# A mixture-of-experts layer in split fp32: one first-layer piece unsplit for light experts, another order of experts, longer rows in the second-layer loads

## The chip, the cores and the metric

One core of a Trainium2 chip runs the whole layer in one launch. The metric is the device time of one execution in microseconds (us), the median of three runs. TensorE (PE) multiplies, VectorE (DVE) and ScalarE (ACT) work on elements, GpSimd (POOL) issues indirect transfers, SyncE (SP) issues the weight loads.

## The reference, cut to what matters

The layer mixes 512 tokens of width 1024 (state-space heads and pooling heads), and then sends each token through 4 of 32 experts. Everything is fp32, and the 384 MiB of expert weights are read once.

```python
logits = xt @ router_w + router_b            # 512 tokens, 32 experts
top_val, top_idx = lax.top_k(logits, 4)
gates = softmax(top_val)
# for each expert e, on the tokens sent to it:
hb = x @ w1[e] + b1[e]                       # 1024 -> 2048
g = minimum(hb[..., ::2], 7);  u = clip(hb[..., 1::2], -7, 7)
act = g * sigmoid(1.702 * g) * (u + 1)       # 1024
y = (act @ w2[e] + b2[e]) * gate             # 1024 -> 1024, added into the token's row
x = x + g2 * sum_of_y;  out = rmsnorm(x, final_norm_w)
```

## The kernel before, in words

**Split products.** An fp32 product is made of reduced fp32 (F32R) ones. A piece of weights, a tile `raw` of 128x2048 and 1 MiB, is split by `ring_split` (L1070): ScalarE rounds it to `hi` (L1076), VectorE subtracts, `lo = raw - hi` (L1077). There are three hi/lo pairs. The tokens of an expert are split in the same way. `prod` (L1299) multiplies 128 rows of weights: hi·hi, lo·hi and hi·lo, on four PSUM halves of 512 columns in the first layer and on two in the second.

**Light and wide experts.** The kernel ranks the experts by their number of tokens at run time (`order`, L1427). Positions 0 and 1 hold experts 0 and 1 with 128 slots each; the other positions follow `RANK` (L48), and `CAPS` (L50) gives the slots of each. Ranks 15 to 29 are light, 64 slots (`LT`): their 64 hi columns and 64 lo columns stand side by side in one stationary operand of 128 columns, so `prod` needs two products where a wide expert (80 to 128 slots) needs three. Rows 64 to 127 of the result hold what the lo columns gave; `rest` (L1273) copies them to `b2h`, and a product with the strip `slt` adds them, along with the bias, to rows 0 to 63 (`bias1` L1281, `bias2` L1291). Position `MID` (16) holds the fullest expert, rank 0, with a block of 128 and one of 64 slots; it runs in a branch of its own, without overlap with its own second layer. All others alternate wide and light after the first three.

**The loop over positions** (L1523). At position p: eight pieces of the first layer, `w1_piece(e, k)`, each 128 rows of 8192 bytes. Ahead of the second piece, the second-layer bias and the scatter of position p-2 (`end`); behind the third, the gather and transposition of the next expert's rows (`next_x`). Then `selector(p)` writes the one-hot columns that pick the expert's row of the biases: for a wide expert a tile `sel` of 128x128, `SELB` (2) buffers; for a light one the strip `slt`, of which columns 0 and 2 serve the first-layer bias, column 1 the second-layer bias, column 3 the rest. Then the bias and `swiglu` (L1308: Gelu on ACT to `sg`, clamp on DVE to `su`, product to `act`), with which the four PSUM halves (two tiles A, two buffers in all) come free for the next first layer. Between them, in `C` (L1344), the second layer of position p-1 in four loads `w2_pair(e, kk)`: rows 256kk to 256kk+127 in the left half of the tile, the next 128 in the right half, so a partition gets two rows of 4096 bytes. Last, `act` is transposed by PE, eight blocks of 128 columns (L1109 light, L1119 wide), for the second layer one position later.

**Buffers and queues.** The loads go through a ring of 11 `raw` buffers, in order, on SP's queue (L1064); a load waits for its buffer. Gathers (L1099) and scatters (L1328) are on POOL's queue. Every engine runs its instructions in an order that is fixed when the program is built; a tile of a pool may be written anew when all readers of the one that had its buffer are through.

Of the kernel before, what the change touches and what calls it, by code (L numbers as in the profile page):

```python
# [16 lines left out]
P = 128  # L17
# [28 lines left out]
LT = 64  # L46
MID = 16
RANK = [30, 31] + [1, 15, 2, 16, 3, 17, 4, 18, 5, 19, 6, 20, 7, 21, 0, 22, 8, 23, 9, 24, 10, 25, 11, 26, 12, 27, 13, 28,  # L48
                   14, 29]
CAPS = [(128,), (128,)] + [(LT,) if r > 14 else (128, LT) if r == 0 else (128,) if r < 5 else (112,) if r < 9 else  # L50
# [47 lines left out]
def mixer_and_moe(tc, a):  # L98
# [996 lines left out]
    def w2_pair(e, kk):  # L1095
        return pair(of_expert(a["w2"][0], e), kk)

# [5 lines left out]

    def transposed(src, m, pool, name, bufs, tbank):
        if m == LT:
            both = pool.tile([P, KT, 2, LT], F32R, name=name + "h", tag=name + "h", bufs=bufs)
            tp = tbank()
            for k in range(KT):
                PE.transpose(tp[:, k * LT:(k + 1) * LT], src[0:LT, k * P:(k + 1) * P], ident[0:LT, 0:LT])  # L1109
            v = tp.rearrange("p (k t) -> p k t", k=KT)  # L1110
            SC.activation(both[:, :, 0, :], v, AF.Copy)
            VE.tensor_tensor(both[:, :, 1, :], v, both[:, :, 0, :].bitcast(F32), op=ALU.subtract)  # L1112
            return (both.rearrange("p k i t -> p k (i t)"),)
        hi = pool.tile([P, KT, P], F32R, name=name + "h", tag=name + "h", bufs=bufs)
        lo = pool.tile([P, KT, P], F32R, name=name + "l", tag=name + "l", bufs=bufs)
        for h in range(2):
            tp = tbank()
            for k in range(4):
                PE.transpose(tp[:, k * P:k * P + m], src[0:m, (h * 4 + k) * P:(h * 4 + k + 1) * P],  # L1119
                             ident[0:m, 0:m])  # L1120
            o = hi[:, h * 4:(h + 1) * 4, 0:m]
# [46 lines left out]
XDB = 3  # L1168
SELB = 2
SUB = 1  # L1170
# [24 lines left out]
LEAD = 3  # L1195
ORDER_AT = 3
LIMIT = 7.0
ALPHA = 1.702
# [4 lines left out]
def moe(tc, a, c_, cst, psa, psb, phx, pc, pd, g2, b1h, b2h, msum, gate, rkm, tab, ixa, last, table_out, acc_scr, halfneg,  # L1203
# [34 lines left out]
    def gathered(col, m):  # L1238

        nx[0] += 1  # L1240
        t = xgs[nx[0] % 2]
        if nx[0] > 1:
            gather_(t, col, m)
        return transposed(t, m, "x", 1, (pc, phx)[nx[0] % 2])

    def transposed(src, m, name, bufs, pool=None):
        return transposed_(src, m, pool or phx, name, bufs, lambda: bank("T"))

# [8 lines left out]
    def selector(p):  # L1257
        if CAPS[p][-1] == LT:
            SC.activation(slt[0:LT, 0:2, :], selm[0][0:LT, p:p + 1].unsqueeze(2).broadcast_to([LT, 2, LT]), AF.Copy)
            SC.activation(slt[LT:P, 2, :], selm[0][LT:P, p:p + 1].broadcast_to([LT, LT]), AF.Copy)  # L1260
            if len(CAPS[p]) == 1:
                return True
# [9 lines left out]

    def rest(banks):  # L1273

        if len(banks) == 1:
            SC.activation(b2h[LT:P, :], banks[0][LT:P, :], AF.Copy)
# [22 lines left out]
    def prod(banks, m, x, k, hi, lo, last=False):  # L1299
# [3 lines left out]
        for i, (u, v) in enumerate(ps):  # L1303
            for j, bk in enumerate(banks):
                PE.matmul(bk[0:n, :], lhsT=u[:, k, 0:n], rhs=v[:, j * 512:(j + 1) * 512], start=(k == 0 and i == 0),  # L1305
                          stop=((last or m == LT and k == KT - 1) and v is lo))

    def swiglu(t, m, out, plus=0.0):  # L1308
# [35 lines left out]
    def C(p, blocks, sl=None, hooks=()):  # L1344
# [13 lines left out]
        for (act, m, gcol, icol), bk in zip(blocks, bks):  # L1358
            if m == LT:
                rest(bk)  # L1360

# [161 lines left out]
    for p in range(E):  # L1523
        e = ids[p] = expert(p)
        m = CAPS[p][0]
        if p != MID:
# [3 lines left out]
            for k in range(KT):  # L1530
                hi, lo = lead[k] if p == 0 and k < LEAD else split(load(w1_piece(e, k)))
                prod(bks, m, x, k, hi, lo)
                if k == 0 and end is not None:
# [31 lines left out]
        else:  # L1565
# [3 lines left out]
            for h in range(2):  # L1569
                two = [bank("B") for _ in range(2)]  # L1570
                for kk in range(KT // 2):
# [5 lines left out]
                    if h == 0 and kk == 1:  # L1577
                        end()
                        end = C(*pend)
# [64 lines left out]
    if m == LT:  # L1644
        rest(bk)
    bias2(bk, m, sl)
# [109 lines left out]
```

## Time and profile before

| | us |
|---|---|
| median of three runs | 1806.4 (1801.19 to 1806.83) |
| the profiled execution | 1804.47 |
| its span, first to last instruction | 1802.7 |
| PE busy | 1635.2 (91%) |
| DVE busy | 1541.8 (86%) |
| ACT busy | 1168.1 (65%) |
| POOL busy | 621.0 (34%) |

A busy time is that of one engine, and the engines overlap: the shares say how full an engine was, not what the time is made of. The mean granted TensorE clock was 0.964 of full speed. PE's matmuls are pipelined, so that a busy PE need not be at its peak.

### The profile page before, as it was taken

The page shows a single profiled execution, that of the slowest core. Times are in us where ns is not written, and L with a number is a line of the kernel's source. Part 1 is how long each engine was busy: PE and PEld are TensorE (multiplying, and loading weights), DVE is VectorE, ACT ScalarE, POOL GpSimd, SP SyncE. Part 2 cuts the span into 40 slices and gives each one's busy share as a digit, 9 for nine tenths or more (in the row PEclk, how much of TensorE's full clock was granted, in tenths as well). Part 3 has the DMA queues.
Part 4 walks back from the last instruction along what each step waited for, and adds up shares of the span by engine and source line. Part 5 has one row for each costly group of instructions (what it writes and reads, how often), then busy time and mean ns, then how long its engine had stood idle before and what let it go on. Part 6 is the DMA issues. An engine that isn't in the chain of part 4 may idle for free. (4 is left out here: it accounts for less than half of the span.)

```text
span 1802.7 us, 21388 instructions
## 1 busy us (share of the span) xinstructions
PE 1635.2 (91%) x7371; PEld 1197.1 (66%) x7371; DVE 1541.8 (86%) x1491; ACT 1168.1 (65%) x1204; POOL 621.0 (34%) x288
## 2 busy tenths in 40 slices
PE   6998889998899799999999999998999998999985
PEld 2776667676677577767667667676666666666653
DVE  7767888987878989999989998966899999999994
ACT  6445336556643467787777877755778777787773
POOL 1303456779210102242540531501053363313303
PEclk8999899999999889999999999999999999999996
DMA  9646443223577779999999999985899999999953
GB/s 350 200 127 206 150 154 105 101 82 106 191 249 304 258 289 365 363 388 384 362 388 392 356 380 401 351 304 197 341 385 384 380 365 365 390 374 374 384 222 102
DMA packets 138561, 521.53 MB, mean 289 GB/s; under 512 B 14919, under 2 KB 45063, under 8 KB 106704
## 3 DMA queue, kind: packets, MB, share of 16 engines
q1 hardware_dynamic: 125446, 490.39, 71.6%
q0 software_dynamic: 6880, 16.79, 4.0%
q10 hardware_dynamic: 6122, 12.94, 2.1%
q8 instruction: 59, 0.97, 0.2%
q14 instruction: 54, 0.44, 0.1%
HBM read 508.78 MB, written 18.37 MB: 292 GB/s over the span
## 5 line engine op out<-in xcount | busy, mean ns | idle before, releaser
L1077 DVE TENSOR_TENSOR lo<-raw,hi 128x2048 fp32r<-128x2048 f32 x398 | 897.4, 2283 | 88.5 <-ACT hi L1076 85.5
L1076 ACT ACTIVATE hi<-raw 128x2048 fp32r<-128x2048 f32 x398 | 752.0, 1915 | 180.7 <-PE A L1305 106.7
L1328 POOL DMA_INDIRECT acc_scr<-y,ixi x32 | 239.9, 7498 | 531.2 <-DVE y L1326 450.8
L1305 PE MATMUL A<-lo,xh 128*128 128x512 f32 (+3 forms) x1072 | 310.9, 407 | 37.5 <-DVE lo L1077 32.8
L1305 PE MATMUL A<-hi,xh 128*128 128x512 f32 (+3 forms) x1072 | 304.4, 400 | 7.0 <-ACT hi L1076 3.8
L1305 PEld LDWEIGHTS A<-lo,xh 128*128 128x128 f32 (+3 forms) x1072 | 184.3, 181 | 126.9 <-DVE lo L1077 80.0
L1305 PEld LDWEIGHTS A<-hi,xh 128*128 128x128 f32 (+3 forms) x1072 | 192.2, 182 | 62.8 <-ACT hi L1076 5.6
L1099 POOL DMA_INDIRECT xg<-h_scr,ixi x30 | 114.7, 3823 | 269.4 <-PE S L1109 150.2
L1305 PE MATMUL S<-lo,ah 128*128 128x512 f32 (+3 forms) x512 | 165.8, 404 | 15.4 <-DVE lo L1077 15.3
L1305 PE MATMUL S<-hi,ah 128*128 128x512 f32 (+3 forms) x512 | 165.6, 403 | 3.8 <-DVE ah L1112 3.8
L1305 PE MATMUL A<-hi,xl 128*128 128x512 f32 (+3 forms) x544 | 153.8, 396 | 0.0
L1305 PEld LDWEIGHTS S<-lo,ah 128*128 128x128 f32 (+3 forms) x512 | 90.5, 183 | 49.8 <-DVE lo L1077 24.2
L1305 PEld LDWEIGHTS A<-hi,xl 128*128 128x128 f32 (+3 forms) x544 | 95.0, 175 | 31.4
L1305 PEld LDWEIGHTS S<-hi,ah 128*128 128x128 f32 (+3 forms) x512 | 92.6, 184 | 33.2 <-DVE ah L1112 4.0
L228 ACT ACTIVATE hi<-raw 128x1024 fp32r<-128x1024 f32 (+1 forms) x73 | 75.9, 1045 | 40.0 <-PE A L355 14.3
L231 DVE TENSOR_TENSOR lo<-raw,hi 128x1024 fp32r<-128x1024 f32 (+1 forms) x59 | 77.8, 1322 | 18.6 <-ACT hi L228 17.4
L1305 PE MATMUL S<-hi,al 128*128 128x512 f32 (+3 forms) x272 | 86.2, 396 | 0.0
L630 ACT ACTIVATE row<-row,nb 128x128 f32<-128x128 f32 x192 | 59.5, 389 | 37.4 <-POOL row L626 37.3
L336 PE MATMUL A<-hx,hi 128*128 128x512 f32 x160 | 65.8, 411 | 3.4 <-DVE at L378 2.1
L338 PE MATMUL A<-hx,lo 128*128 128x512 f32 x160 | 66.2, 414 | 0.0
L337 PE MATMUL A<-hx,hi 128*128 128x512 f32 x160 | 65.2, 408 | 0.0
L378 DVE SCALAR_TENSOR_TENSOR at<-A,cw,at 128x510 f32<-128x510 f32 (+1 forms) x80 | 57.8, 740 | 5.9 <-ACT at L374 5.4
(452 smaller groups left out, 2476.1 us busy)
## 6 DMA issues: line engine op xcount, KB each, us to landing
raw<-in_w_dram SPq DMA_DIRECT2D x384, 1024.0 KB
raw<-in_w_in_dram SPq DMA_DIRECT2D x36, 512.0 KB
mraw<-in_w_mod_dram SPq DMA_DIRECT2D x32, 512.0 KB
raw<-in_w_out_dram SPq DMA_DIRECT2D x14, 1024.0 KB
row<-cs_scr ACTq DMA_DIRECT2D x32, 384.0 KB
raw<-in_w_mod_dram SPq DMA_DIRECT2D x16, 512.0 KB
raw<-in_w_in_dram SPq DMA_DIRECT2D x16, 384.0 KB
xt<-in_x_dram SPq DMA_DIRECT2D x4, 512.0 KB
```

What stands on the lines that cost most here:

```text
L228: SC.activation(hi, r, AF.Copy)
L231: e.tensor_tensor(lo, r, hi.bitcast(F32), op=ALU.subtract)
L336: PE.matmul(lat, lhsT=hi[:, k, :], rhs=row_of(hxh, k), start=(k == 0), stop=False)
L337: PE.matmul(lat, lhsT=hi[:, k, :], rhs=row_of(hxl, k), start=False, stop=False)
L338: newest[0] = PE.matmul(lat, lhsT=lo[:, k, :], rhs=row_of(hxh, k), start=False, stop=(k == KT - 1))
L378: VE.scalar_tensor_tensor(ac[:, u:v], src[:, u + o:v + o], cw[:, j, ct:ct + 1], ac[:, u:v], op0=ALU.mult, op1=ALU.add)
L630: SC.activation(row[:, h, :], row[:, h, :], AF.Exp, bias=nb[:, c, i:i + 1])
L1076: ia = SC.activation(hi, r, AF.Copy)
L1077: i = VE.tensor_tensor(lo, r, hi.bitcast(F32), op=ALU.subtract)
L1099: PO.indirect_dma_start(out=t[0:m, :], out_offset=None, in_=h2_scr, in_offset=bass.IndirectOffsetOnAxis(ap=col[0:m, :], axis=0), bounds_ch ...
L1305: PE.matmul(bk[0:n, :], lhsT=u[:, k, 0:n], rhs=v[:, j * 512:(j + 1) * 512], start=(k == 0 and i == 0), stop=((last or m == LT and k == KT ...
L1328: PO.indirect_dma_start(out=acc_scr, out_offset=bass.IndirectOffsetOnAxis(ap=icol[0:m, :], axis=0), in_=y[0:m, :], in_offset=None, bounds_ ...
```

## The change

Four edits and what they need:

- **One piece unsplit.** Light experts take piece `WHOLE_K` (4) of the first layer as it is: PE multiplies the fp32 `raw` tile with an fp32 copy `xw` of the tokens' columns (`prod_whole`), onto rows 0 to 63 of the four PSUM halves. `transposed` makes that copy where it transposes the tokens of a 64-slot block.
- **Longer rows.** `w2_pair` gives partition p the rows 2p and 2p+1 of its 256, one run of 8192 bytes. So that the products match, `act` is transposed from every second column (`paired`).
- **Order.** `MID` is 6: behind positions 0 and 1 come four light experts, the fullest, a light one, and then ten groups of one or two wide experts with a light one behind each: `RANK` is 30, 31, 15, 16, 17, 18, 0, 19, 1, 20, 2, 21, 3, 4, 22, 5, 23, 6, 7, 24, 8, 25, 9, 26, 10, 11, 27, 12, 28, 13, 14, 29.
- **Selectors.** As light experts now follow each other, column 1 of `slt` is written in `rest`, at the end of the second layer, and no longer in `selector`. `SELB` is 1: one buffer for `sel`.

```diff
@@ -44,9 +44,11 @@
 LT = 64
-MID = 16
-RANK = [30, 31] + [1, 15, 2, 16, 3, 17, 4, 18, 5, 19, 6, 20, 7, 21, 0, 22, 8, 23, 9, 24, 10, 25, 11, 26, 12, 27, 13, 28,
-                   14, 29]
+MID = 6
+FULL, LIGHT = list(range(1, 15)), list(range(15, 30))
+RANK = [30, 31] + LIGHT[0:4] + [0, LIGHT[4]]
+for i_ in range(10):
+    RANK += FULL[i_ * 14 // 10:(i_ + 1) * 14 // 10] + [LIGHT[5 + i_]]
 CAPS = [(128,), (128,)] + [(LT,) if r > 14 else (128, LT) if r == 0 else (128,) if r < 5 else (112,) if r < 9 else
                            (96,) if r < 13 else (80,) for r in RANK[2:]]
@@ -1093,7 +1095,8 @@
         return pair(of_expert(a["w1"][0], e)[:, h * FF:(h + 1) * FF], kk)
     def w2_pair(e, kk):
-        return pair(of_expert(a["w2"][0], e), kk)
+        return of_expert(a["w2"][0], e)[2 * kk * P:2 * (kk + 1) * P, :].rearrange("(p k) n -> p (k n)", k=2)
     def gather(t, col, m):
         PO.indirect_dma_start(out=t[0:m, :], out_offset=None, in_=h2_scr,
@@ -1101,23 +1104,31 @@
                               bounds_check=T - 1, oob_is_err=False)
         return t
-    def transposed(src, m, pool, name, bufs, tbank):
+    def transposed(src, m, pool, name, bufs, tbank, paired=False):
+        def tile_of(k):
+            return src[0:m, k // 2 * 2 * P + k % 2:(k // 2 + 1) * 2 * P:2] if paired else src[0:m, k * P:(k + 1) * P]
         if m == LT:
             both = pool.tile([P, KT, 2, LT], F32R, name=name + "h", tag=name + "h", bufs=bufs)
             tp = tbank()
             for k in range(KT):
-                PE.transpose(tp[:, k * LT:(k + 1) * LT], src[0:LT, k * P:(k + 1) * P], ident[0:LT, 0:LT])
+                PE.transpose(tp[:, k * LT:(k + 1) * LT], tile_of(k), ident[0:LT, 0:LT])
             v = tp.rearrange("p (k t) -> p k t", k=KT)
             SC.activation(both[:, :, 0, :], v, AF.Copy)
             VE.tensor_tensor(both[:, :, 1, :], v, both[:, :, 0, :].bitcast(F32), op=ALU.subtract)
-            return (both.rearrange("p k i t -> p k (i t)"),)
+            if name != "x":
+                return (both.rearrange("p k i t -> p k (i t)"),)
+            one = pc.tile([P, LT], F32, name="xw", tag="xw", bufs=2)
+            SC.activation(one, v[:, WHOLE_K, :], AF.Copy)
+            return both.rearrange("p k i t -> p k (i t)"), one
         hi = pool.tile([P, KT, P], F32R, name=name + "h", tag=name + "h", bufs=bufs)
         lo = pool.tile([P, KT, P], F32R, name=name + "l", tag=name + "l", bufs=bufs)
         for h in range(2):
             tp = tbank()
             for k in range(4):
-                PE.transpose(tp[:, k * P:k * P + m], src[0:m, (h * 4 + k) * P:(h * 4 + k + 1) * P],
-                             ident[0:m, 0:m])
+                PE.transpose(tp[:, k * P:k * P + m], tile_of(h * 4 + k), ident[0:m, 0:m])
             o = hi[:, h * 4:(h + 1) * 4, 0:m]
             v = tp.rearrange("p (k t) -> p k t", k=4)[:, :, 0:m]
             SC.activation(o, v, AF.Copy)
@@ -1166,7 +1177,7 @@
 XDB = 3
-SELB = 2
+SELB = 1
 SUB = 1
 SGB = 2
 H2T = 0
@@ -1194,6 +1205,7 @@
 TAIL = 2
 LEAD = 3
 ORDER_AT = 3
+WHOLE_K = 4
 LIMIT = 7.0
 ALPHA = 1.702
@@ -1241,10 +1253,11 @@
         t = xgs[nx[0] % 2]
         if nx[0] > 1:
             gather_(t, col, m)
-        return transposed(t, m, "x", 1, (pc, phx)[nx[0] % 2])
+        return transposed_(t, m, (pc, phx)[nx[0] % 2], "x", 1, lambda: bank("T"))
     def transposed(src, m, name, bufs, pool=None):
-        return transposed_(src, m, pool or phx, name, bufs, lambda: bank("T"))
+        return transposed_(src, m, pool or phx, name, bufs, lambda: bank("T"), True)
@@ -1256,7 +1269,7 @@
     def selector(p):
         if CAPS[p][-1] == LT:
-            SC.activation(slt[0:LT, 0:2, :], selm[0][0:LT, p:p + 1].unsqueeze(2).broadcast_to([LT, 2, LT]), AF.Copy)
+            SC.activation(slt[0:LT, 0, :], selm[0][0:LT, p:p + 1].broadcast_to([LT, LT]), AF.Copy)
             SC.activation(slt[LT:P, 2, :], selm[0][LT:P, p:p + 1].broadcast_to([LT, LT]), AF.Copy)
             if len(CAPS[p]) == 1:
                 return True
@@ -1270,8 +1283,11 @@
     def halves(t):
         return [t[:, 0:512], t[:, 512:1024]]
-    def rest(banks):
+    def rest(banks, p=None):
+        if p is not None:
+            SC.activation(slt[0:LT, B2, :], selm[0][0:LT, p:p + 1].broadcast_to([LT, LT]), AF.Copy)
         if len(banks) == 1:
             SC.activation(b2h[LT:P, :], banks[0][LT:P, :], AF.Copy)
         else:
@@ -1304,6 +1320,11 @@
             for j, bk in enumerate(banks):
                 PE.matmul(bk[0:n, :], lhsT=u[:, k, 0:n], rhs=v[:, j * 512:(j + 1) * 512], start=(k == 0 and i == 0),
                           stop=((last or m == LT and k == KT - 1) and v is lo))
+    def prod_whole(banks, x, r):
+        for j, bk in enumerate(banks):
+            PE.matmul(bk[0:LT, :], lhsT=x, rhs=r[:, j * 512:(j + 1) * 512], start=False, stop=False)
     def swiglu(t, m, out, plus=0.0):
@@ -1357,7 +1378,7 @@
             return bks
         for (act, m, gcol, icol), bk in zip(blocks, bks):
             if m == LT:
-                rest(bk)
+                rest(bk, p)
         def end():
             for (act, m, gcol, icol), bk in zip(blocks, bks):
@@ -1528,8 +1549,11 @@
             two = [bank("B") for _ in range(2)]
             bks = [b for t in two for b in halves(t)]
             for k in range(KT):
-                hi, lo = lead[k] if p == 0 and k < LEAD else split(load(w1_piece(e, k)))
-                prod(bks, m, x, k, hi, lo)
+                if m == LT and k == WHOLE_K:
+                    prod_whole(bks, x[1], load(w1_piece(e, k)))
+                else:
+                    hi, lo = lead[k] if p == 0 and k < LEAD else split(load(w1_piece(e, k)))
+                    prod(bks, m, x, k, hi, lo)
                 if k == 0 and end is not None:
                     end()
                     end = None
@@ -1575,7 +1599,8 @@
                         for j in range(2):
                             prod(halves(two[j]), ms[j], xs[j], 2 * kk + i, hi[:, q], lo[:, q])
                     if h == 0 and kk == 1:
-                        end()
+                        if end is not None:
+                            end()
                         end = C(*pend)
                     if h == 0 and kk == 2:
                         end()
@@ -1642,7 +1667,7 @@
     for c in range(NT - LATE_HI):
         others(c)
     if m == LT:
-        rest(bk)
+        rest(bk, p)
     bias2(bk, m, sl)
     y = finish(bk, m, gcol, icol)
     yh, yl = [half(F32R) for _ in range(2)]
```

## Rows read from the trace of the kernel before

**Rows 1.** Windows of 100 us: busy time of each engine, clock, DMA.

```profile
core 0: us, PE busy (x) PEld busy (x) DVE busy (x) ACT busy (x) POOL busy (x), PEclk, DMA share, GB/s
...
700.00:800.00 100.00, 96.30 (x426) 72.15 (x424) 93.77 (x65) 78.88 (x58) 22.72 (x5) 1.00 0.99 382
...
1200.00:1300.00 100.00, 89.47 (x382) 64.77 (x381) 66.36 (x47) 57.16 (x46) 10.70 (x5) 0.95 0.67 243
```

**Rows 2.** Groups by line, 740 to 1160: names, shapes, count, busy us, mean ns.

```profile
L1077 DVE TENSOR_TENSOR lo<-raw,hi 128x2048 fp32r<-128x2048 f32 x144 | 324.1, 2283 | 24.9 <-ACT hi L1076 24.0 <-DMA raw<-in_w_dram 0.9
L1076 ACT ACTIVATE hi<-raw 128x2048 fp32r<-128x2048 f32 x144 | 271.6, 1916 | 41.8 <-PE A L1305 26.7 <-PE S L1305 4.4 <-DMA raw<-in_w_dram 4.1
...
L1305 PE MATMUL A<-hi,xh 128*128 128x512 f32 (+1 forms) x384 | 106.6, 396 | 0.8 <-ACT hi L1076 0.8
...
L1119 PEld LDWEIGHTS S<-con,act 128*128 128x128 f32 (+1 forms) x48 | 5.8, 140 | 1.7
...
L1109 PEld LDWEIGHTS S<-con,act 64*128 64x128 f32 x48 | 4.1, 138 | 3.8 <-issue 2.6 <-DVE y L1326 0.7
...
L1260 ACT ACTIVATE slt<-selm 64x64 fp32r<-64x64 f32 x7 | 1.8, 252 | 0.5 <-PE A L1287 0.3
...
L1267 DVE CAST sel<-selm 128x128 fp32r<-128x128 f32 x6 | 1.3, 210 | 0.0
```

**Rows 3.** Windows, columns as above: the stretch, a wide and a light first layer.

```profile
740.00:1160.00 420.00, 395.52 (x1741) 289.51 (x1741) 389.00 (x260) 322.68 (x244) 155.38 (x24) 1.00 0.99 377
...
957.60:980.30 22.70, 22.69 (x99) 16.57 (x96) 21.39 (x13) 17.40 (x10) 1.56 (x1) 1.00 1.03 386
990.90:1013.00 22.10, 18.98 (x80) 13.12 (x79) 21.61 (x15) 18.31 (x16) 18.11 (x2) 1.00 0.90 343
```

**Rows 4.** Waits in 740 to 1160: total us, times, longest.

```profile
PEld A L1305 <- DVE lo L1077: 37.0, 46, 1.9
...
ACT hi L1076 <- DMA raw<-in_w_dram: 4.1, 1, 4.1
...
SPq L1064 <- DVE lo L1077: 336.0, 144, 4.8
```

**Rows 5.** Windows of 10 us, columns as above: clock and DMA rate.

```profile
630.00:640.00 10.00, 8.20 (x21) 6.09 (x22) 8.41 (x12) 7.23 (x6) 2.56 (x2) 0.52 0.87 315
975.00:985.00 10.00, 10.00 (x46) 7.36 (x45) 7.70 (x6) 6.72 (x6) 0.00 (x0) 1.00 1.01 422
...
995.00:1005.00 10.00, 7.34 (x29) 4.75 (x28) 10.00 (x7) 9.74 (x8) 9.70 (x2) 1.00 0.76 271
...
1220.00:1230.00 10.00, 9.12 (x33) 6.94 (x34) 2.85 (x5) 1.12 (x3) 0.00 (x0) 0.66 0.31 113
```

**Rows 6.** PE's timeline, a wide first layer, then a light one: start, length.

```profile
957.66 1.18 PE L1305 MATMUL A<-hi,xh 128*112 128x512 f32 x4
...
979.29 1.09 PE L1305 MATMUL A<-lo,xh 128*112 128x512 f32 x4
...
1002.55 1.20 PE L1305 MATMUL A<-lo,xh 128*128 128x512 f32 x4 [1.15 <-DVE lo L1077]
...
1004.76 1.20 PE L1305 MATMUL A<-lo,xh 128*128 128x512 f32 x4
...
1006.96 1.20 PE L1305 MATMUL A<-lo,xh 128*128 128x512 f32 x4
```

**Rows 7.** DVE's timeline: splits without a gap.

```profile
1029.94 15.50 DVE L1077 TENSOR_TENSOR lo<-raw,hi 128x2048 fp32r<-128x2048 f32 x7 [0.63 <-ACT hi L1076]
```

**Rows 8.** The fp32 products of line 1640: ns min, median, max; starts.

```profile
L1640 PE MATMUL A<-raw,con x4: 592/592/667, 1770.9 to 1772.3; 128*128 128x512 f32 x4
```

**Rows 9.** PE's timeline between positions 0 and 1.

```profile
627.84 1.23 PE L1289 MATMUL A<-b1h,sel 64*128 64x512 f32 x4
...
631.80 1.22 PE L1305 MATMUL A<-hi,xh 128*128 128x512 f32 x2 [1.85 <-DVE su L1319]
```

## The prediction

> **What bounds the kernel now.** I read the windows of 100 us first [rows 1]. From 700 us on they are alike: PE 96%, DVE 94%, DMA share 0.99 in 700 to 800; only 1200 to 1300, around the fullest expert, falls to 0.67 and 243 GB/s. Nothing in that table says which of the three sets the pace, so I took a steady stretch, 740 to 1160, and asked who waits for whom. It holds 144 splits [rows 2], that is 12 experts in 420 us, 35.0 us each, half of them light.
>
> The stream of weights looks full (share 0.99, 377 GB/s [rows 3]), yet ScalarE waited for a landed piece once, for 4.1 us, in 144 splits; SyncE waited 336 us for VectorE to hand a buffer back [rows 4]. The pieces lie ready and the ring is waiting for the splits. Where nothing indirect shares the engines they moved 422 GB/s, and just after, with issues held back, 271 at a share of 0.76 [rows 5]: there is some room, not much.
>
> Between PE and DVE the pace changes hands. In the first layer of a wide expert PE runs without a gap: 24 groups of four products start 0.94 us apart (957.66 to 979.29 is 23 steps), 0.235 us a product [rows 6]; the window shows PE 22.69 of 22.70 us, DVE 21.39 [rows 3]. In the first layer of a light expert PE starts the lo products every 2.20 us (1002.55, 1004.76, 1006.96), which is VectorE's pace: seven splits in a row took 15.50 us, 2.21 each [rows 6, 7]. Eight products need 1.88 us, so PE starves: in 990.9 to 1013.0 DVE was busy 21.61 of 22.10 us and PE 18.98 [rows 3], and over the stretch PE's weight loads waited 37.0 us for lo in 46 cases [rows 4], 6.2 us for each of the six light experts. So a light expert costs what VectorE needs for it, a wide one what PE needs. That is the stage in which the change must be priced.
>
> **The change part by part.** *The unsplit piece.* Each of the 15 light experts loses one of twelve splits: 2.21 us of DVE and 1.9 of ACT [rows 2]. PE replaces 8 products (1.88 us) by four in full fp32. The trace has that form at the end, L1640: two instructions for each product, 0.592 us long against 0.396 for a split one [rows 2, 8]. Their extra 0.196 us on a step of 0.235 gives 0.43; their starts (1770.9 to 1772.3 in three steps) give 0.47. Eight of them are 3.4 to 3.7 us, so PE gains 1.6 to 1.9 us of work. Does it fit where PE starves? The light window loses 2.2 of 22.1 us and leaves 19.9. PE's own work there is 64 products, 15.0, with some 1.4 for two bias products and eight transposes of the next rows: 16.4, and 18.2 after. It fits with 1.7 us to spare, and while PE is at the long piece VectorE fills the three hi/lo pairs. Bounds for a light expert: a gain of 2.2 if VectorE paces it throughout, of 0.4 if PE does from there on (2.2 less 1.8). The wait rows are near the first end; I take 2.0, and 15 × 2.0 = 30 us.
>
> *What it adds on ScalarE:* a copy of 128x64, one more fill of the selector strip in rest, one fill made narrower; each about 0.25 us (L1260 [rows 2]), less than the 1.9 it loses. ScalarE is busy 323 of 420 us [rows 3]: nothing on the path. If it were the pace, the edit would still gain 1.4 us an expert. The buffer of the unsplit piece is handed back by PE, not by VectorE, at most three pieces later. Behind that wait on SP's queue stand all later loads; as the pieces lie ready [rows 4] I price it at nothing; were the stream the pace, each would cost its delay, some microseconds.
>
> *Runs of 8192 bytes.* The second-layer loads issue the same number of transfers, with half the rows. No row times the two kinds apart; with the stream off the path the price is nothing either way, and if it were the pace the upper end is the difference between 377 and 422 GB/s [rows 3, 5] on a third of the bytes, 1.2 us an expert. The price it asks for is in the transposes: L1109 and L1119 now load every second column of act. The present loads take 0.14 us each [rows 2], eight an expert. Lower bound no change; upper bound, as if each read took twice as long, 1.1 us an expert, on PE where a wide expert is PE-paced (17 × 1.1 = 19 us). Weight loads overlap products, so I take 0. The Trainium skill (SBUF — State Buffer, Door 1: The DMA port swizzle) has it that fp32 reads may step up to the point where two still fall in one 16-byte line; a step of two elements does, so by it the price is 0 also; no run here shows such a load yet.
>
> *The order.* The fullest expert costs about 36 us of stream ((1 - 243/377) × 100 us [rows 1, 3]) because PE alone has 240 products for twelve pieces. It stands between two light ones before and after, so the sum only moves. Four light experts in a row take a piece every 2.7 us or so ((35 - 2)/12 and less), about what 422 GB/s gives (1.05 MB in 2.5), and a full ring stands ready behind the first two wide ones: no price. After it, wide experts come in four pairs.
>
> *One buffer for the wide selector (SELB).* That is the part that speaks against the change. The tile sel of a wide expert is read by its first-layer bias and, one expert later, by its second-layer bias. With one buffer, the next wide expert can't fill its own until the second-layer bias of the one before is through, so its bias, swiglu, and thereby the release of the four PSUM halves come behind the whole second layer instead of ahead of it. PE then has no banks for the next first layer. This happens where two wide experts are neighbours: positions 0 and 1, and the four pairs, five places. The price of one: the fill 0.21 (L1267 [rows 2]); from the end of the bias products to the first product of the next expert, at a place where nothing covered it, 627.84 + 1.23 to 631.80, 2.7 us, ended by su [rows 9]; and up to one split, 2.2, ahead of the fill on VectorE's queue. 2.9 to 5.1, middle 4.0. Queued behind the fill on DVE are splits, but three pairs lie filled. All five are followed by a light expert, whose first layer then starts with three pieces split, so PE makes up the 1.7 us spare there: 2.3 net, 5 × 2.3 = 11.5 us. If the clock falls in the gap, as it did behind the gaps ahead of 631.8 (0.52 granted over 630 to 640) and in 1220 to 1230 (0.66) [rows 5, 9], that is 3.4 to 4.8 us more a place (0.34 and 0.48 of 10 us).
>
> **Sum.** The profiled execution took 1804.5 us (span 1802.7). 1804.5 - 30 + 11.5 = 1786. The median of the runs is 1.9 us above the profiled one, so 1788 us.
>
> **The rivals.** *The stream is the pace after all.* For it: share 0.99. Against: one wait for data in 144 splits, and 422 GB/s in places. If so, the gain stops at the room left: 1 to 1.5% of the 1,050 us from 700, 10 to 16 us, so 1790 to 1796, and with the selector's stalls hidden behind it. The Trainium skill (DMA: Bandwidth & Descriptors, Specifications) gives a core about 358 GB/s from HBM; by that rule an expert's 12.58 MB take 35.1 us, an estimate from that page that happens to equal the pace here, and the change would give nothing, 1806. The trace disagrees: 422 GB/s stood for 10 us at a time [rows 5].
>
> *The selector's buffer eats the gain* (the other side). Place: the five neighbourhoods. With 5.1 us, nothing made up, and 3.4 for the clock, 8.5 × 5 = 42 us: 1804.5 - 30 + 42 + 1.9 = 1819. It decides from 6.0 us a place. For it: the chain at 627 to 632 is that long already, and the clock fell there. Against: a light expert follows each time, with VectorE ahead.
>
> *PE becomes the bound of the light experts* too: the gain drops to 0.4 each, 6 us, against 11.5 for the stalls: 1812. For it: PE busy 395 of 420 us [rows 3]. Against: busy is not full, 46 waits for lo.
>
> *No stalls, full gain:* 15 × 2.2 = 33 and the ring refilled early by the fullest expert: 1773.
>
> **Chances and range.** Forecast (1778 to 1800) 0.56; full gain 0.09; the stream 0.12; the selector 0.15; PE 0.08. What a measurement of this kernel tells from no change is 0.3%, 5.4 us: faster means under 1801, slower over 1812. Faster: 0.56 + 0.09 + three quarters of the stream's, less what the forecast leaves near its edge, 0.69. Slower: most of the selector and half of PE, 0.15. Same 0.16. The range reaches to the full gain, 1772, and to the selector's case short of its end, 1812.
>
> **What would show it.** Right: 384 - 15 = 369 splits of 128x2048 in this stage; in a light first layer eight fp32 instructions 0.4 to 0.5 us apart and PE's waits for lo down from 6 us to under 3 an expert; light windows of about 20 us; at five places PE idle 3 to 5 us ahead of a light expert's first product, ended by su, with L1267 behind L1297. Wrong: ScalarE waiting for raw often (the stream); no idle time at those places, or over 6 us with a clock of 0.5; transposes with weight loads near 0.28 us; light windows still at 22 us.

## The result: 1.2% slower, and the profile after

The changed kernel takes 1826.1 us (median of four runs, 1824.6 to 1827.6) against 1804.4 beside it: a ratio of 1.012, interval 1.0107 to 1.0133. The forecast was 1788, the range 1772 to 1812, and slower had a chance of 0.15. The time is 14 us above the upper end.

In the steady stretch 740 to 1160 the windows of the changed kernel (columns as in [rows 1]; the second row is a place that is read below) show VectorE 353 us busy where [rows 3] have 389. With the new order other experts lie in this stretch (five wide and between seven and eight light ones, six and six before), so its sums show where the engines wait and not what a kernel gained.

```profile
740.00:1160.00 420.00, 397.89 (x1696) 293.55 (x1695) 353.24 (x241) 300.02 (x249) 92.54 (x24) 0.98 0.91 354
1130.00:1134.00 4.00, 4.00 (x13) 3.20 (x13) 3.84 (x4) 0.00 (x0) 0.47 (x1) 0.61 0.84 269
```

The same stretch by waits (total us, times, longest):

```profile
ACT hi L1078 <- PE A L1321: 51.2, 36, 4.4
DVE lo L1079 <- ACT hi L1078: 31.3, 34, 2.9
...
PEld A L1321 <- DVE lo L1079: 9.5, 13, 1.5
...
PE A L1321 <- DVE lo L1079: 5.0, 6, 1.2
```

PE's weight loads wait 9.5 us for lo, where [rows 4] had 37.0. But PE is as busy as before (398 us, 396 in [rows 3]), and 128 pieces are split in place of 144. The queue turned round: ScalarE now waits 51.2 us for PE to give a `hi` buffer back, and VectorE 31.3 us for ScalarE (26.7 and 24.0 in [rows 2]).

And by lines (columns as in [rows 2]). L1327 is the unsplit product, L1116 and L1131 are the transposes, with `act` read in steps of two elements and `xg` contiguous:

```profile
L1079 DVE TENSOR_TENSOR lo<-raw,hi 128x2048 fp32r<-128x2048 f32 x128 | 288.5, 2283 | 32.2 <-ACT hi L1078 31.3 <-DMA raw<-in_w_dram 0.4
...
L1327 PE MATMUL A<-raw,xw 128*64 128x512 f32 x48 | 21.9, 598 | 0.0
...
L1131 PEld LDWEIGHTS S<-con,act 128*128 128x128 f32 x40 | 6.4, 203 | 2.7 <-DVE act L1341 2.0
...
L1131 PEld LDWEIGHTS S<-con,xg 128*128 128x128 f32 (+1 forms) x48 | 5.5, 141 | 0.8
```

A weight load of `act` takes 0.203 us, where [rows 2] have 0.140 and the contiguous `xg` beside it still takes 0.141.

A place where two wide experts are neighbours, in PE's timeline (start, length, what it is, idle before it). The third row is the next expert's first product:

```profile
1124.74 0.73 PE L1313 MATMUL S<-b2h,sel 64*128 64x512 f32 x2
1126.22 0.74 PE L1305 MATMUL A<-b1h,sel 64*128 64x512 f32 x4 [0.75 <-DVE sel L1280]
1129.67 1.22 PE L1321 MATMUL A<-hi,xh 128*128 128x512 f32 x2 [2.72 <-DVE su L1340]
1130.69 1.05 PE L1321 MATMUL A<-lo,xh 128*128 128x512 f32 x2
1131.55 1.05 PE L1321 MATMUL A<-hi,xh 128*128 128x512 f32 x2
```

Only when the second-layer bias has read `sel` (1124.74) can the next fill start, then come bias, swiglu and the release of the banks: PE idles 0.75 and 2.72 us, and afterwards its pairs of products start 0.86 and 1.02 us apart where two products need 0.47, at a granted clock of 0.61 (window 1130 to 1134 above). All five places look so: the gap that su ends is 2.7 us long at four of them and 5.0 at the last, and over the four us behind it the granted clock is 0.50 to 0.63. The same place with two buffers is shown under sel2.

The unsplit piece itself, at another light expert, earlier in the same timeline:

```profile
963.95 1.21 PE L1321 MATMUL A<-lo,xh 128*128 128x512 f32 x4 [1.24 <-DVE lo L1079]
965.08 3.65 PE L1327 MATMUL A<-raw,xw 128*64 128x512 f32 x8
968.66 1.20 PE L1321 MATMUL A<-hi,xh 128*128 128x512 f32 x4
```

Its eight instructions take 3.58 us from start to start, the size that was forecast (3.4 to 3.7). PE was idle for lo just ahead of it.

### The profile page after: what moved, and what is told of

It is laid out like the page before. It is cut to its first block, busy times and chain, and to the rows that moved or that the text cites. A ratio compares the mean times of both kernels' runs of the same rounds, so it can differ in the third digit from the quotient of the medians.

```text
span 1824.0 us, 21364 instructions
## 1 busy us (share of the span) xinstructions
PE 1661.6 (91%) x7371; PEld 1209.0 (66%) x7371; DVE 1510.0 (83%) x1476; ACT 1144.8 (63%) x1222; POOL 524.8 (29%) x288
## 2 busy tenths in 40 slices
DMA packets 122177, 521.53 MB, mean 286 GB/s; under 512 B 14919, under 2 KB 45063, under 8 KB 73936
## 3 DMA queue, kind: packets, MB, share of 16 engines
q1 hardware_dynamic: 109062, 490.39, 70.3%
## 5 line engine op out<-in xcount | busy, mean ns | idle before, releaser
L1079 DVE TENSOR_TENSOR lo<-raw,hi 128x2048 fp32r<-128x2048 f32 x383 | 864.7, 2284 | 117.8 <-ACT hi L1078 108.3
L1078 ACT ACTIVATE hi<-raw 128x2048 fp32r<-128x2048 f32 x383 | 724.2, 1915 | 195.9 <-PE A L1321 134.2
L1349 POOL DMA_INDIRECT acc_scr<-y,ixi x32 | 167.0, 5218 | 553.2 <-DVE y L1347 442.4
L1321 PE MATMUL A<-hi,xh 128*128 128x512 f32 (+3 forms) x1012 | 299.7, 408 | 22.6 <-DVE su L1340 18.0
L1321 PE MATMUL A<-lo,xh 128*128 128x512 f32 (+3 forms) x1012 | 295.0, 405 | 15.8 <-DVE lo L1079 15.4
L1321 PEld LDWEIGHTS A<-hi,xh 128*128 128x128 f32 (+3 forms) x1012 | 182.6, 186 | 88.1 <-DVE su L1340 21.0
L1102 POOL DMA_INDIRECT xg<-h_scr,ixi x30 | 93.5, 3115 | 355.2 <-PE S L1116 193.1
```

The costliest lines, as they stand in the source:

```text
L1078: ia = SC.activation(hi, r, AF.Copy)
L1079: i = VE.tensor_tensor(lo, r, hi.bitcast(F32), op=ALU.subtract)
L1102: PO.indirect_dma_start(out=t[0:m, :], out_offset=None, in_=h2_scr, in_offset=bass.IndirectOffsetOnAxis(ap=col[0:m, :], axis=0), bounds_ch ...
L1349: PO.indirect_dma_start(out=acc_scr, out_offset=bass.IndirectOffsetOnAxis(ap=icol[0:m, :], axis=0), in_=y[0:m, :], in_offset=None, bounds_ ...
```

## Experiments

Theories for the 21.6 us. **A**: the one selector buffer costs far more than 2.3 us a place. **B**: the unsplit piece makes PE the pace. **C**: the order costs (wide neighbours, light ones in a row). **D**: the strided weight loads hold PE up. **E**: only the piece and the selector cost, because PE has no room for the piece's 1.7 us. All ratios are to the kernel before, run on the same chip (1803.1 to 1805.5 us), with their intervals.

**First four: parts taken out of the changed kernel.** sel2 gives the selector its second buffer (three small tiles move to another pool for the room); alt_sel1 takes the old order; alt_sel2 has both; nowhole splits every piece and leaves out the copy `xw`.

```diff
-SELB = 1                                  # sel2, alt_sel2
+SELB = 2
-MID = 6                                   # alt_sel1, alt_sel2: MID and RANK of before
+MID = 16
-                if m == LT and k == WHOLE_K:      # nowhole
+                if False:
```

> The changed kernel with two buffers for the wide selector again (three small tiles moved to other pools to make room). Theory A (the single selector buffer ate the gain at the five places where wide experts are neighbours): about 1781 us, 1772 to 1790, and PE's waits for su at line 1340 (18 us) gone. Theory B (the unsplit piece makes PE the pace of the light experts): 1815 to 1826. Theory C (the order itself, wide experts in pairs): 1815 to 1826.

> The changed kernel with the order of before (fullest at 16, wide and light alternating); one selector buffer. Theory A: only two places are left (positions 0 to 2), so about 1790 us, 1782 to 1796. Theory B: 1810 or more. Theory C: 1774 to 1785.

> The order of before and two selector buffers; the unsplit piece and the runs of 8192 bytes stay. Theory A and theory C: 1774 to 1780 (15 times 2 us under before). Theory B: 1810 or more.

> The changed kernel with all first-layer pieces split as before; new order, one selector buffer and long runs stay. Theory A and theory C: the 30 us of the light experts are lost on top, 1845 to 1856. Theory B: 1800 to 1810.

| | us | ratio |
|---|---|---|
| sel2 | 1810.3 | 1.0035 (1.0022 to 1.0048) |
| alt_sel1 | 1821.1 | 1.0098 (1.0076 to 1.0121) |
| alt_sel2 | 1816.1 | 1.0063 (1.0045 to 1.0081) |
| nowhole | 1834.5 | 1.0170 (1.0145 to 1.0194) |

The second buffer gives 15.8 us back in the new order (five neighbouring places, 3.2 each) and 5.1 in the old one (two places, 2.5 each). PE's timeline of sel2 at the place shown above:

```profile
1121.57 0.73 PE L1313 MATMUL S<-b2h,sel 64*128 64x512 f32 x2
1122.22 1.20 PE L1321 MATMUL A<-hi,xh 128*128 128x512 f32 x4
...
1129.99 1.19 PE L1321 MATMUL A<-lo,xh 128*128 128x512 f32 x4 [1.13 <-DVE lo L1079]
...
1132.72 1.19 PE L1321 MATMUL A<-lo,xh 128*128 128x512 f32 x4 [0.61 <-DVE lo L1079]
```

From the second-layer bias to the next first product it is 0.65 us there and 4.93 with one buffer: 4.3 us later. The lower clock behind it costs another 1.6: eight products take 3.5 us (1129.67 to 1133.19) that need 1.9. PE makes up 1.7 of it, the two waits for lo that sel2 has behind the place and the changed kernel has not. Added up that is 4.2 us, and by the start of the first-layer bias products the changed kernel lies 4.0 us further behind sel2 past this place than ahead of it (8.6 at 1259.86, 4.6 at 1080.92). But with two buffers the kernel still isn't faster than before, so the 30 us of the unsplit piece are missing as well. nowhole shows 8.4 us for it here. All four runs lie outside the ranges of A and of C; B's hold for alt_sel1 and alt_sel2 and fail for sel2 and nowhole.

**Next four: parts put alone onto the kernel before** (two selector buffers, old order, column 1 of `slt` filled in `rest` as in the changed kernel; `best` has the new order, and with the unsplit piece the three small tiles move as in sel2). w2only has the long rows and the strided transposes, runsonly the long rows with contiguous transposes, wholeonly the unsplit piece, best the unsplit piece in the new order.

```diff
-        return pair(of_expert(a["w2"][0], e), kk)                      # w2only, runsonly
+        return of_expert(a["w2"][0], e)[2 * kk * P:2 * (kk + 1) * P, :].rearrange("(p k) n -> p (k n)", k=2)
-        return transposed_(src, m, pool or phx, name, bufs, lambda: bank("T"))          # w2only
+        return transposed_(src, m, pool or phx, name, bufs, lambda: bank("T"), True)
```

> The kernel before with the runs of 8192 bytes and their transposes of every second column; pieces split, order and two selector buffers as before (the selector strip is still filled in rest). Theory D (the strided weight loads of the transposes, 0.205 us against 0.140 in the profile of the changed kernel, delay PE, which paces the kernel): 8 x 0.065 = 0.5 us an expert, 1810 to 1822. Theory E (only the unsplit piece and the selector buffer cost something): 1800 to 1808.

> As w2only, but act transposed from neighbouring columns as before (the second layer then meets the rows of w2 in another order, so this part of the computation is changed): the long runs alone. Theory D: 1800 to 1808, at or a little under before. A theory by which the long runs themselves disturb the stream: as slow as w2only.

> The kernel before with the unsplit piece alone; loads of 4096-byte runs, order and two selector buffers as before. As the prediction had it (VectorE paces the light experts): 1774 to 1782. Theory E (PE has no room for the 1.7 us that the piece adds): 1804 to 1815. Theory D: 1790 to 1805.

> The changed kernel with two selector buffers and the loads and transposes of before: new order and unsplit piece stay. Theory D: sel2's 1810 less 10 to 17, 1793 to 1801, under before. Theory E: 1808 to 1812.

| | us | ratio |
|---|---|---|
| w2only | 1811.2 | 1.0041 (1.0027 to 1.0054) |
| runsonly | 1805.3 | 1.0004 (0.9992 to 1.0016) |
| wholeonly | 1806.4 | 1.0012 (1.0003 to 1.0021) |
| best | 1803.5 | 0.9993 (0.9982 to 1.0004) |

Longer rows are worth nothing; reading `act` in steps of two costs 5.9 us (w2only less runsonly), and 6.8 in the new order (sel2 less best, the longer rows included). The lines of w2only, 740 to 1160:

```profile
L1113 PE MATMUL S<-con,act 64*128 64x64 f32 x48 | 7.9, 285 | 0.0
L1113 PEld LDWEIGHTS S<-con,act 64*128 64x128 f32 x48 | 6.9, 208 | 3.6 <-issue 2.6 <-DVE y L1344 0.7
```

and of runsonly, where the step is one:

```profile
L1113 PE MATMUL S<-con,act 64*128 64x64 f32 x52 | 5.8, 232 | 0.0
L1113 PEld LDWEIGHTS S<-con,act 64*128 64x128 f32 x52 | 4.4, 138 | 4.1 <-issue 2.6 <-DVE y L1344 0.7 <-DVE sel L1277 0.4
```

So D holds beside A. The piece alone gives nothing (+1.8), but B's price, 1.7 us on each of 15 experts, does not show either; something gives and something takes. `best` lies between the ranges of D (1793 to 1801) and E (1808 to 1812).

**What the unsplit piece gives and takes.** Three kernels on wholeonly change the work of one engine at a time: wholehalf multiplies the unsplit piece into two PSUM halves, splitkeep keeps the split and drops the products, wholesplit does the split on top. The theories are F, PE is the pace of a light expert; G, PE and VectorE share it; H, VectorE is the pace. orderonly is the new order with all pieces split.

```diff
-        for j, bk in enumerate(banks):              # wholehalf, in prod_whole
+        for j, bk in enumerate(banks[0:2]):
-                    prod_whole(bks, x[1], load(w1_piece(e, k)))
+                    split(load(w1_piece(e, k)))     # splitkeep
-                    prod_whole(bks, x[1], load(w1_piece(e, k)))
+                    r_ = load(w1_piece(e, k))       # wholesplit
+                    prod_whole(bks, x[1], r_)
+                    split(r_)
```

> The kernel before with the unsplit piece of the light experts, but multiplied into two of the four PSUM halves only (the other half of that piece's contribution is left out). An unsplit piece costs TensorE 3.58 us where the split one cost 1.88; half of it costs 1.79, so TensorE's work is that of before and VectorE's is 2.2 us less per light expert. F, TensorE is already the pace of a light expert: no change, 1800 to 1807. G, both engines share the pace and a saved microsecond on either counts in part (the unsplit piece alone gave 0 because 1.7 us more on one cancelled 2.2 less on the other): 10 to 20 us faster, 1785 to 1795. H, VectorE paced it and only the extra 1.7 us took the gain: 15 x 2.0 = 30 us faster, 1775.

> The kernel before where the light experts still split piece 4 of the first layer but leave out its products: TensorE loses 8 products, 1.88 us per light expert, VectorE and ScalarE nothing. F: 15 x 1.9 = 28 us faster, 1776. G: 10 to 18 us faster. H, VectorE is the pace: within 5 us of before.

> The kernel before with the unsplit piece, and the split of that piece made all the same, its result unused: TensorE has 1.7 us more per light expert, VectorE as much as before. F: 15 x 1.7 = 25 us slower, 1830. G: 10 to 18 us slower. H: up to the spare time, so 0 to 5 us slower.

> The kernel before with the new order of experts alone: two selector buffers, every piece split, the old second-layer loads and transposes. With the new order, the unsplit piece and two buffers, but the old loads, the time was 1803.5; the unsplit piece alone cost 1.8 us. If the two simply add: 1801 to 1803. If the new order needs the unsplit piece (four light experts in a row starve for VectorE without it): 1808 to 1815. If the order is a gain that the piece ate: under 1798.

| | us | ratio |
|---|---|---|
| wholehalf | 1786.0 | 0.9891 (0.9874 to 0.9908) |
| splitkeep | 1811.0 | 1.0037 (1.0024 to 1.0049) |
| wholesplit | 1812.4 | 1.0040 (1.0026 to 1.0053) |
| orderonly | 1806.6 | 1.0015 (1.0004 to 1.0026) |

None of F, G and H fits all three. wholehalf, with less work for VectorE and no more for PE, gains 18.5 us, as G has it and short of H's 30; splitkeep, with less for PE alone, gains nothing (against F and G); wholesplit loses 7.9, between H's 0 to 5 and G's 10 to 18. orderonly lies between its three ranges too; the order costs 2.1 us. The time of a pair, one wide and one light expert, can be read off the fills of `sel`, one for each wide expert: instructions of that tile on VectorE from 860 to 1130 (ns min, median, max; first and last start). Before, three pairs in 209.5 us, 69.8 each:

```profile
L1267 DVE CAST sel<-selm x4: 208/208/210, 888.7 to 1098.2; 128x128 fp32r<-128x128 f32 x4
```

wholeonly, 70.3:

```profile
L1277 DVE CAST sel<-selm x4: 206/207/210, 888.1 to 1099.0; 128x128 fp32r<-128x128 f32 x4
```

wholehalf, 68.6:

```profile
L1277 DVE CAST sel<-selm x4: 207/208/210, 884.5 to 1090.4; 128x128 fp32r<-128x128 f32 x4
```

Taking 1.79 us of products from wholeonly shortens the pair by 1.7: behind the unsplit piece PE is the pace, and the split that it saves is worth only 69.8 less 68.6, 1.2 us. In these three pairs wholesplit says the same from the other side (210.1 / 3, 70.0 us, with the split back); as a whole it is 6.0 us slower than wholeonly, so elsewhere the split is not free. splitkeep came out slower with less to do. Its PE timeline and a window behind the longer wait:

```profile
1001.58 1.21 PE L1318 MATMUL A<-lo,xh 128*128 128x512 f32 x4 [1.16 <-DVE lo L1076]
...
1005.99 1.82 PE L1318 MATMUL A<-lo,xh 128*128 128x512 f32 x4 [2.27 <-DVE lo L1076]
...
1012.29 0.63 PE L1318 MATMUL S<-hi,ah 128*112 128x512 f32 x2
1006.00:1010.00 4.00, 4.00 (x11) 3.14 (x12) 4.00 (x2) 1.91 (x1) 4.00 (x1) 0.57 1.00 422
```

Where the fifth piece's products were, PE waits 2.27 us for the sixth piece's lo, and the granted clock behind that wait is 0.57: from the fourth piece's lo to the end of the layer it is 10.71 us, 9.85 before (1002.55 to 1012.40). So the clock falls in four of the six light layers from 740 to 1160 (0.57 to 0.62 over four us). In the layer where the same wait ends at 936.27 the clock stays at 1.00, and there the stretch takes 9.85 us (931.87 to 941.72) as before: the products left out there were worth nothing, and with every piece split VectorE is the pace up to the layer's end, as H has it.

**Is it a balance?** If a pair costs the larger of PE's 68.6 and VectorE's 69.8 us, a quarter unsplit is the best share. part1 and part2 split 1536 and 1024 of the piece's 2048 columns and leave one and two PSUM halves to `prod_whole`; part1n is the first in the new order.

```diff
-                    prod_whole(bks, x[1], load(w1_piece(e, k)))
+                    r_ = load(w1_piece(e, k))
+                    hi, lo = split(r_, 1536)
+                    prod(bks[0:3], m, x, k, hi, lo)
+                    prod_whole(bks, x[1], r_)       # on the last bank alone
```

> The kernel before, and of piece 4 of a light expert three quarters (1536 columns) are split and multiplied as before, the last quarter (one PSUM half) goes unsplit. TensorE gains 0.45 us of work per light expert, VectorE loses 0.55. Balance (a pair takes the larger of TensorE's 68.6 and VectorE's 69.8 us in steady alternation): 69.05 against 69.25, so 0.5 us a pair less than before, 15 x 0.5 = 8 us faster, 1797. Fixed cost of an unsplit piece: 1805 to 1810. VectorE alone as the pace (the prediction): also 8 us.

> The same with half of the piece unsplit. TensorE gains 0.85 us per light expert, VectorE loses 1.1. Balance: 69.45 against 68.7, 0.35 us a pair less than before, 5 us faster, 1800, and behind the quarter. Fixed cost: 1805 to 1810. VectorE alone as the pace: 15 x 1.1 = 16 us faster, 1788, ahead of the quarter.

> The quarter in the new order of experts, with two selector buffers and the old second-layer loads and transposes. With all pieces split this order gave 1806.6, with the whole piece unsplit 1803.5. Balance: 5 to 9 us below the first, 1798 to 1802. Fixed cost: 1804 to 1807.

1796.9 us (0.9954, 0.9938 to 0.9969), 1799.9 (0.9969, 0.9955 to 0.9983) and 1802.0 (0.9990, 0.9978 to 1.0001). The balance forecast the first two within 0.2 us and the third at the edge of its range (1798 to 1802), and a fixed cost of any unsplit piece is out. And yet PE's 68.6 us are not PE's need, as its timeline shows. The first layer of the same light expert, before (the first and second piece's lo, the fifth piece's hi, and the second layer's first product at the end):

```profile
992.40 1.10 PE L1305 MATMUL A<-lo,xh 128*128 128x512 f32 x4
...
997.09 1.20 PE L1305 MATMUL A<-lo,xh 128*128 128x512 f32 x4 [1.36 <-DVE lo L1077]
...
1003.59 1.09 PE L1305 MATMUL A<-hi,xh 128*128 128x512 f32 x4
...
1012.40 0.63 PE L1305 MATMUL S<-hi,ah 128*112 128x512 f32 x2
```

and in wholeonly:

```profile
992.18 1.08 PE L1318 MATMUL A<-lo,xh 128*128 128x512 f32 x4
...
996.86 1.20 PE L1318 MATMUL A<-lo,xh 128*128 128x512 f32 x4 [1.37 <-DVE lo L1076]
...
1002.33 1.20 PE L1318 MATMUL A<-lo,xh 128*128 128x512 f32 x4 [1.14 <-DVE lo L1076]
1003.46 3.65 PE L1324 MATMUL A<-raw,xw 128*64 128x512 f32 x8
1007.03 1.20 PE L1318 MATMUL A<-hi,xh 128*128 128x512 f32 x4
...
1012.67 0.62 PE L1318 MATMUL S<-hi,ah 128*112 128x512 f32 x2
```

PE's long waits, 1.37 and 1.14 us, lie ahead of the lo of the second and the fourth piece and are the same in both kernels. The fifth piece comes after them. From there to the end of the layer the four pieces took 8.81 us before (1003.59 to 1012.40) and take 9.21 now: 3.57 for the unsplit one and 5.64 for the three others, 1.88 each. Four split pieces at 1.88 are 7.5 us, so PE had 1.3 us to spare there, and the unsplit piece adds 1.7. With half of its products the same stretch takes 7.49 us (998.25 to 1005.74 in wholehalf), 1.3 less than before: that is the 1.2 us a pair that the saved split is worth. Hence a last rival to the balance: the piece lies at the wrong place.

**The place.** whole_k1 is wholeonly, after_k1 the changed kernel and best_k1 `best`, with the second piece unsplit.

```diff
-WHOLE_K = 4
+WHOLE_K = 1
```

> The kernel before with the unsplit piece alone (two selector buffers, old order, old second-layer loads), and the unsplit piece is the second of the eight instead of the fifth. Place: TensorE takes its 3.6 us where it now sits idle (1.4 us ahead of the second piece's lo products, 1.1 ahead of the fourth's), and the last lo is ready one split, 2.2 us, earlier; the first layer ends 2.0 to 2.3 us earlier than before, 15 x 2 = 30 us, 1775 (1770 to 1785). Balance alone (a pair can't fall below TensorE's own work, as with the fifth piece): 1802 to 1808.

> The changed kernel with only the place of the unsplit piece altered, second instead of fifth. Place: about 2 us less for each of 15 light experts, some less where two wide experts come ahead of it and VectorE has caught up: 20 to 30 us off 1826, so 1796 to 1806. Balance alone: 1822 to 1830.

> The changed kernel with two selector buffers, the old second-layer loads and transposes, and the unsplit piece second. From the changed kernel with the piece second (1815.6): one selector buffer cost 16 us and the strided transposes 6 to 7, so 1793. If the order is neutral also here, the piece's place gives what it gave in the old order, 24 us off the same kernel with the piece fifth (1803.5): 1780 to 1783. In the new order seven of the light experts stand behind two wide ones or among their like and showed no stall ahead of the second piece there; if so 1790 to 1795.

| | us | ratio |
|---|---|---|
| whole_k1 | 1782.8 | 0.9884 (0.9868 to 0.9899) |
| after_k1 | 1815.6 | 1.0057 (1.0045 to 1.0070) |
| best_k1 | 1782.9 | 0.9881 (0.9865 to 0.9898) |

One constant takes 23.6 us off wholeonly and 20.6 off best. whole_k1 and best_k1 lie in the ranges of the place (1770 to 1785, 1780 to 1783); after_k1 lies in neither of its two (1796 to 1806, 1822 to 1830). PE's timeline of the same expert in whole_k1:

```profile
987.91 1.09 PE L1318 MATMUL A<-lo,xh 128*128 128x512 f32 x4
988.92 3.65 PE L1324 MATMUL A<-raw,xw 128*64 128x512 f32 x8
992.50 0.99 PE L1128 MATMUL S<-con,xg 112*128 112x112 f32 x8
993.26 1.18 PE L1318 MATMUL A<-hi,xh 128*128 128x512 f32 x4
...
998.31 1.20 PE L1318 MATMUL A<-lo,xh 128*128 128x512 f32 x4 [0.17 <-DVE lo L1076]
...
1005.95 0.62 PE L1318 MATMUL S<-hi,ah 128*112 128x512 f32 x2
```

From the first piece's lo to the end of the layer it is 18.04 us, 20.49 in wholeonly and 20.00 before. PE multiplies the raw tile while VectorE makes the two lo that it used to wait for, and in this layer no wait for lo above 0.17 us is left. The pair takes 67.7 us (203.0 / 3):

```profile
L1277 DVE CAST sel<-selm x4: 208/209/210, 886.7 to 1089.7; 128x128 fp32r<-128x128 f32 x4
```

That is less than the 68.6 which the balance took for PE's need, with 1.8 us more products than wholehalf has: the balance is refuted as a cause, although it met two runs. Its 68.6 contained PE's waits ahead of the fifth piece. whole_k1 and best_k1 are faster than both kernels.

## Why the prediction was wrong

**The step that failed** is "Does it fit where PE starves? … It fits with 1.7 us to spare", and with it "I take 2.0, and 15 × 2.0 = 30 us". The long piece's price was right (3.58 us for 3.4 to 3.7), the split saved was right, and PE did starve for lo. But PE's idle time was added up over the whole first layer, as if a piece anywhere in it could use all of it; the most of it lies ahead of the lo of the second and the fourth piece, and the unsplit one is the fifth. Behind those waits PE had 1.3 us to spare, and the piece adds 1.7. A gain of 2.0 was forecast; 1.2 for the split less 1.7 for the long piece was measured, 0.5 us a pair lost in the steady pairs, and 1.8 us in all (some other pairs gained), where −30 stood. Where the piece lies second, the forecast's sum holds: 69.8 less 67.7 is 2.1 us a pair, and 22 us were measured (the steady pair's 2.1 is not reached at every light expert). [Rows 6] could have told it: they carry the wait [1.15 <-DVE lo] on the fourth piece's lo and none on the next two, and from there PE's step of 2.20 us against the 1.88 of eight products leaves 0.32 a piece, 1.3 over the last four. The 37.0 us of waits in [rows 4] are those of weight loads, which lie in part under products still running; PE's own waits for lo on the same line came to 15.3 us in 14 cases.

**The rival that came closest** was "PE becomes the bound of the light experts": a gain of 0.4 each, 0.08 of the chance. It is right for the pieces from the fifth on, wrong for the layer.

**The selector's buffer** was the part named as speaking against the change, with the right mechanism and the right five places; the term was mis-sized. Its gross price of 4.0 us a place was measured as 4.3, and the 1.7 that PE was to make up was made up at the place shown. Net it was 3.2 a place and 15.8 us in all, not 2.3 and 11.5: the fall of the clock, which the prediction named at 3.4 to 4.8 us a place and left out of the sum, came at all five places and cost 1.6 at the one shown.

**The strided transposes** were priced at 0 with an upper end of 1.1 us an expert; 5.9 to 6.8 us over 32 experts is 0.2 each. Eight loads at 0.065 us more are 0.5, so some of it is hidden. "Weight loads overlap products, so I take 0" failed. The Trainium skill (SBUF — State Buffer, Door 1: The DMA port swizzle), by which a step of two fp32 elements costs nothing, is contradicted here: 0.203 to 0.209 us against 0.138 to 0.141.

**What was to be seen.** Eight fp32 instructions 0.45 us apart, L1280 behind L1313 with gaps ended by su, and waits of weight loads for lo down to a fourth came as written; the light windows of about 20 us that were to follow from the last did not: with the piece fifth the layer followed above grew from 20.00 to 20.49 us.

**Right at 0**: the longer rows (+0.7 us, within their interval) and, nearly, the order (orderonly +2.1, just clear of no change; best_k1 equal to whole_k1). The stream was not the pace: whole_k1 moves 384 GB/s over 740 to 1160, where [rows 3] have 377, and carries the same bytes in 22 us less.

**The account**, as a chain of kernels from before to after: order +2.1 (orderonly), unsplit piece −3.1 (best less orderonly, the moved tiles included), strided transposes and long rows +6.8 (sel2 less best), one selector buffer +15.8 (after less sel2). The kernel before itself reads 1803.1 to 1805.5 us beside these runs, so a term is known to about 2 us and the two small ones hardly differ from nothing. That they add up to 21.6 is so by construction; that the terms depend on each other is seen in the piece (+1.8 alone, −3.1, −8.4 in the changed kernel) and the selector (5.1 at two places in the old order). What stays open: in the changed kernel the better place is worth only 10.4 us, and between after_k1 and best_k1 lie 32.7 us where the selector and the transposes cost 22.6 with the piece fifth; how the 10 us more divide between the two was not measured. The traces show where they arise. By the start of the first-layer bias products after_k1 lies 10.8 us behind best_k1 past the four light experts at the start (843.34) and 25.1 past the third place (1439.02); with the piece fifth the changed kernel lies 5.0 and 15.4 us behind `best` there. In the alternating stretch between the first place and the second both distances grow alike, by 1.6 and 1.9 us. Behind the first and the last gap of after_k1 the unsplit piece itself runs at the lower clock: its first four instructions take 3.47 and 3.68 us (683.50 and 1733.78), 1.93 elsewhere.

## What to carry to other kernels

Where one engine's idle time is to pay for its extra work, find where in the stage the idle time lies, row by row in its timeline, and put the work ahead of that point; an average over the stage can't tell. Read the wait of the engine itself, not that of its overlapped loads, and look also at a step that is longer than the work in it: the rest is idle time that no wait shows. A model that meets two runs may still name the wrong cause: the run that moves one constant and no work told it apart. A buffer taken from a tile that is read one stage later costs a whole chain wherever two users become neighbours, and here the clock behind the gap as well.

## What the runs showed of the hardware that was not expected

Reading an fp32 operand in steps of two elements lengthened PE's weight loads from 0.138 to 0.208 us and the small products with them from 0.232 to 0.285 (64 rows). Second-layer rows of 8192 bytes in place of 4096 cut the packets from 138,561 to 122,177 and changed no time. Dropping 1.9 us of products for each light expert made the kernel 6.5 us slower: PE stood 2.27 us in their place, and in four of six layers the granted clock fell behind that wait (0.57 over 1006 to 1010; 0.957 against 0.964 over the span).
